# Low parts of the MLP's down weights: adding DMA and ScalarE copy in place of a VectorE subtraction

## Chip, cores and metric

The kernel runs on one core of one Trainium2 chip. The metric is device time in microseconds for one execution, taken as the median of several. The profile is of one more execution, taken by the hardware profiler.

## What is computed

A two-layer trunk over 512 tokens of width 1024, in float32. Layer 0 mixes with a gated linear recurrence, layer 1 with differential attention over a key and value projected once. Each layer ends in the squared-ReLU MLP, the part that the change touches:

```python
def squared_relu_mlp(h, w_up, w_down):
    u = jax.nn.relu(h @ w_up)
    return (u * u) @ w_down
...
ff = squared_relu_mlp(rms_norm(h, mlp_norm_pre[layer]), mlp_w_up[layer], mlp_w_down[layer])
h = h + rms_norm(ff, mlp_norm_post[layer])
```

`w_up` is 1024 x 4096 and `w_down` 4096 x 1024. The result of the MLP goes through an RMS norm with a gain before it is added to the residual stream, so turning the sign of the whole product and the sign of that gain leaves the output as it was.

## The kernel before, in words

**Split products.** TensorE multiplies in the type float32r, which keeps fewer bits than float32. Every operand is therefore held as two float32r tiles: a high part (a rounded copy) and a low part (the original less the high part). `mm3` (L192) makes each product from three matmuls: high by high, high by low, low by high. The third one, in `wmm` (L197), is the first to read the low part of the weights.

**Weights.** `load_w` (L180) brings a weight matrix in tiles of 128 x 1024 float32 (512 KB). `fetch_w` (L150) issues the load on SP's queue into the tile `raw`, of which there are four buffers for all weights. `split_w` (L161) makes the high part `whi` by a ScalarE copy (L167) and the low part `wlo` by a VectorE subtraction (L168). `whi` and `wlo` have eight buffers each. A buffer of `raw` is free again when its subtraction is done, and only then can SP issue the load that is to go into it.

**The MLP.** `block` (L377) goes through the hidden width in four quarters q of 1024 columns. For each it makes the hidden activations `u` (tiles `uhi`, `ulo`, by ScalarE's ReLU, square and copy and VectorE's subtraction) and multiplies them with that quarter of `w_down`: two halves i of 512 columns, four weight tiles each, named dn_q_i_pr.

- q = 0: the up product is plain (`up`, eight PSUM groups, each emptied by ScalarE's ReLU at L405).
- q = 1, 2, 3: four pairs p of `up_pair` (L450), a seven-product scheme. The bank `ux` takes up four products in turn and is read by ScalarE between them: L475 keeps p1 after the first and u2 after the second; L493 reads it for the last time.
- Down product, q = 0, 1, 2 (L513 to L530): half i = 0 goes through the eight row blocks kt with the four output groups n4 inside, so weight tile pr is needed from kt = 2 pr on; half i = 1 has n4 outside and needs all four tiles within its first eighth. Each n4 has a PSUM bank out of the four of the tag "mm". The fourth bank is the one that the last up group of q = 0 (L405), or the last pair's `ux` (L493), used before.
- Down product, q = 3: both halves of weights are loaded and `by_halves` (L358) goes over tokens in two halves, kt outside and eight output groups inside. Groups n = 0 to 3 use the first half's tile, n = 4 to 7 the second half's, so the fifth weight tile, dn_3_1_0, is needed with kt = 0. Groups 6 and 7 are in the bank that `ux` had.

**Order of the work.** TensorE's order is written out by a small planner. On the other engines a scheduler of the framework sets the order, by priorities and a cost model, and each engine then executes its instructions in that order: one that waits holds all behind it. GpSimd (POOL) issues the DMAs of the residual stream (L268, L337) through software-made descriptors; SP issues the weight loads.

Of the kernel before, what the change touches and what calls it, by code (L numbers as in the profile page):

```python
# [9 lines left out]
F32 = mybir.dt.float32  # L10
F32R = mybir.dt.float32r
I32 = mybir.dt.int32
U8 = mybir.dt.uint8
AF = mybir.ActivationFunctionType
# [74 lines left out]
def trunk_kernel(ctx: ExitStack, tc: tile.TileContext, x_t, w_qf, w_g, w_i, w_ao, w_k, w_q, w_v, w_bo, w_up, w_us, w_dn,  # L89
# [50 lines left out]
    ea = cp.tile([P, S], F32, name="ea")  # L140
    gnh = cp.tile([P, G_N], F32, name="gnh")
    v.tensor_scalar(gnh, gn, -0.5, None, op0=ALU.mult)
    epsc = cp.tile([P, 1], F32, name="epsc")
    v.memset(epsc, EPS)
    eps15 = cp.tile([P, 1], F32, name="eps15")
# [15 lines left out]
    def split_w(raw, gain, pr, name):  # L161

        per, ncols = raw.shape[1:]
        hi = wp.tile([P, per, ncols], F32R, tag="whi", name=f"whi_{name}_{pr}", bufs=8)
        lo = wp.tile([P, per, ncols], F32R, tag="wlo", name=f"wlo_{name}_{pr}", bufs=8)
        if gain is None:
            a.activation(hi, raw, AF.Copy)  # L167
            v.tensor_tensor(lo, raw, hi.bitcast(F32), op=ALU.subtract)  # L168
        elif gain.shape[1] == 1:
            a.activation(hi, raw, AF.Copy, scale=gain)  # L170
            v.scalar_tensor_tensor(lo, raw, gain, hi.bitcast(F32), op0=ALU.mult, op1=ALU.subtract)
        else:
            for j in range(per):
                gc = gain[:, per * pr + j:per * pr + j + 1]
                a.activation(hi[:, j, :], raw[:, j, :], AF.Copy, scale=gc)
                v.scalar_tensor_tensor(lo[:, j, :], raw[:, j, :], gc, hi[:, j, :].bitcast(F32),
                                       op0=ALU.mult, op1=ALU.subtract)
        return [(hi[:, j, :], lo[:, j, :]) for j in range(per)]

    def load_w(src, ncols, gain, name):  # L180
        out = []
        for pr in range(ncols // 128):
            out += split_w(fetch_w(src, ncols, pr, name), gain, pr, name)
        return out
# [206 lines left out]
    def block(pool, proj, gpost, name, layer, want):  # L391
# [104 lines left out]
        for q in range(4):  # L496
# [15 lines left out]
                    yield from up_pair(q, p, ts)  # L512
            if q < 3:  # L513
                for i in range(2):
                    wt = load_w(w_dn[layer, q, i], 512, None, f"dn{layer}_{q}_{i}")
                    pss = [mmt(f"dn{layer}_{q}_{i}_{n4}") for n4 in range(4)]
                    if i == 0:
                        order = [(kt, n4) for kt in range(8) for n4 in range(4)]
                    else:
                        order = [(kt, n4) for n4 in range(4) for kt in range(8)]  # L520
                    for kt, n4 in order:
                        wmm(pss[n4], wt, kt, n4 * P, uhi, ulo, 0, S, kt == 0, kt == 7)
                        if kt == 7:
                            n = 4 * i + n4
                            z = zacc[:, n, :]
                            if q == 0:
                                v.tensor_copy(z, pss[n4])
                            else:
                                v.tensor_tensor(z, pss[n4], z, op=ALU.add)  # L529
                        yield 0  # L530
            else:
                wt = [load_w(w_dn[layer, q, i], 512, None, f"dn{layer}_{q}_{i}") for i in range(2)]
                h = 0
                for r in by_halves(wt, uhi, ulo, f"dn{layer}"):
                    if isinstance(r, list):
                        spawn(bounds(pool, r, zacc, h, G_MPOST[layer], ea, want, f"m{layer}"), 0.3)
                        h += 1
                    else:
                        yield r
# [532 lines left out]
```

## Time and profile before

| what | value |
|---|---|
| median of 3 runs | 1291.78 us (1291.08 to 1293.16) |
| profiled execution | 1291.62 us |
| its span | 1289.8 us |
| mean granted TensorE clock | 0.992 |
| DMA, mean over the span | 102 GB/s, 131.01 MB |

The page gives, for each engine, its busy time and share of the span; groups of instructions by line, engine and tiles (written `out<-in`); and DMA issues with the time from issue to landing. The trace also answers with timelines (start, length, engine, line, operation, and in brackets the idle time before it and what ended it), with the chain of work that ended last, and with windows (busy time of each engine, granted clock, share and rate of the DMA engines in a stretch). The profiled execution and its span differ by 1.8 us.

### The profile page before, as it was taken

Reading aid. Unit: us, or ns where it says so; the run is one execution under the profiler, and the core shown is the slowest. Engines: PE = TensorE matmul, PEld = TensorE weight load, DVE = VectorE, ACT = ScalarE, POOL = GpSimd, SP = SyncE. Lnnn points to the kernel's source line nnn. Section 1 sums busy time; section 2 is a strip of 40 time slices with the busy share of each in tenths; the row PEclk is TensorE's granted clock in tenths of the full one; section 3 lists DMA queues with packets and bytes.
Section 4 is the critical chain, followed back from the end, with each engine's and each line's share of the span. In section 5 each row is a group of like instructions: output and inputs, shape, how many; then the busy total and the mean of one; then the engine's idle time right before and its main releaser. Section 6 shows DMA issues by size and latency. Waiting matters only on the chain.

```text
span 1289.8 us, 21392 instructions
## 1 busy us (share of the span) xinstructions
PE 1257.5 (97%) x8450; PEld 1139.5 (88%) x8450; DVE 858.2 (67%) x1791; ACT 663.9 (51%) x1333; POOL 57.4 (4%) x125
## 2 busy tenths in 40 slices
PE   9999999999999999999898999999999999999996
PEld 7989898999988989989898887889998998988995
DVE  7987777648855736647287978674875573764735
ACT  7553535247733715617265887674773370652722
POOL 0210101010000000000100000001000000000000
PEclk9999999999999999999998999999999999999998
DMA  7322222134324512513424432322433151251421
GB/s 241 112 82 66 66 66 74 59 101 152 110 99 74 180 50 66 164 33 119 176 77 155 129 100 65 99 86 78 156 107 99 33 196 33 66 164 47 138 78 66
DMA packets 40166, 131.01 MB, mean 102 GB/s; under 512 B 5089, under 2 KB 7394, under 8 KB 40066
## 3 DMA queue, kind: packets, MB, share of 16 engines
q1 hardware_dynamic: 35072, 113.52, 27.1%
q0 software_dynamic: 4752, 15.99, 4.2%
q8 instruction: 66, 1.08, 0.3%
q14 instruction: 34, 0.28, 0.1%
q10 hardware_dynamic: 242, 0.13, 0.0%
HBM read 119.93 MB, written 9.70 MB: 100 GB/s over the span
## 4 chain that ended last, share of the span: by engine, by line
PE 76%; DVE 11%; ACT 8%; DMA 2%; issue 1%; SPq 0%; DVEq 0%; ACTq 0%
PE dn L114 19%; PE up L114 7%; PE qf L114 7%; PE kq L114 6%; PE dn_h L114 5%; PE g L114 4%; PE ux L114 4%; PE v L114 3%; PE bo_h L114 3%; PE ao_h L114 3%; PE i L114 3%; PE gl L114 3%; DMA raw_dn<-in_w_dn_dram 2%; PE lg L114 2%; ACT r L409 1%
## 5 line engine op out<-in xcount | busy, mean ns | idle before, releaser
L114 PE MATMUL dn<-uhi,whi_dn 128*128 128x512 f32 x384 | 152.0, 396 | 0.0
L114 PE MATMUL dn<-ulo,whi_dn 128*128 128x512 f32 x384 | 151.9, 395 | 0.0
L114 PE MATMUL dn<-uhi,wlo_dn 128*128 128x512 f32 x384 | 151.9, 395 | 0.0
L168 DVE TENSOR_TENSOR wlo_dn<-raw_dn,whi_dn 128x1024 fp32r<-128x1024 f32 x64 | 76.7, 1220 | 18.7 <-ACT whi_dn L167 17.6
L114 PEld LDWEIGHTS dn<-uhi,wlo_dn 128*128 128x128 f32 x384 | 72.1, 188 | 17.5
L114 PEld LDWEIGHTS dn<-uhi,whi_dn 128*128 128x128 f32 x384 | 72.2, 188 | 17.5 <-issue 0.2
L114 PEld LDWEIGHTS dn<-ulo,whi_dn 128*128 128x128 f32 x384 | 72.2, 188 | 17.0
L446 ACT ACTIVATE whi_a<-raw_us 128x1024 fp32r<-128x1024 f32 x24 | 25.3, 1054 | 113.8 <-PE dn L114 113.8
L167 ACT ACTIVATE whi_dn<-raw_dn 128x1024 fp32r<-128x1024 f32 x64 | 67.0, 1054 | 16.5 <-DMA raw_dn<-in_w_dn_dram 12.9
L114 PE MATMUL dn_h<-uhi,whi_dn 128*128 128x256 f32 x240 | 68.7, 286 | 5.8 <-ACT r L493 5.8
L114 PE MATMUL up<-xhi,whi_up 128*128 128x256 f32 x256 | 72.7, 284 | 0.0
L114 PE MATMUL up<-xlo,whi_up 128*128 128x256 f32 x256 | 71.9, 281 | 0.0
L114 PE MATMUL up<-xhi,wlo_up 128*128 128x256 f32 x256 | 71.9, 281 | 0.0
L114 PE MATMUL dn_h<-ulo,whi_dn 128*128 128x256 f32 x240 | 68.1, 284 | 0.0
L114 PE MATMUL dn_h<-uhi,wlo_dn 128*128 128x256 f32 x240 | 68.0, 283 | 0.0
L529 DVE TENSOR_TENSOR zacc<-dn,zacc 128x512 f32<-128x512 f32 x32 | 22.1, 692 | 60.0 <-PE dn L114 59.9
L411 DVE TENSOR_TENSOR ulo<-r,uhi 128x1024 fp32r<-128x1024 f32 (+1 forms) x40 | 40.2, 1010 | 32.4 <-ACT uhi L410 32.4
L114 PE MATMUL ux<-xhi,whi_a 128*128 128x256 f32 x192 | 54.7, 285 | 1.8 <-DVE r L487 1.8
L114 PE MATMUL ux<-xhi,wlo_a 128*128 128x256 f32 x192 | 54.0, 281 | 0.0
L114 PE MATMUL qf<-xhi,whi_qf 128*128 128x512 f32 x128 | 53.2, 416 | 0.7 <-ACT xhi L590 0.7
L114 PE MATMUL ux<-xlo,whi_a 128*128 128x256 f32 x192 | 53.9, 281 | 0.0
L114 PE MATMUL qf<-xlo,whi_qf 128*128 128x512 f32 x128 | 50.8, 397 | 1.0 <-DVE xlo L591 1.0
(368 smaller groups left out, 4075.1 us busy)
## 6 DMA issues: line engine op xcount, KB each, us to landing
raw_dn<-in_w_dn_dram SPq DMA_DIRECT2D x64, 512.0 KB, 4.6
raw_us<-in_w_us_dram SPq DMA_DIRECT2D x48, 512.0 KB, 4.3
raw_up<-in_w_up_dram SPq DMA_DIRECT2D x16, 512.0 KB, 3.6
raw_qf<-in_w_qf_dram SPq DMA_DIRECT2D x15, 512.0 KB, 4.1
raw_wi<-in_w_i_dram SPq DMA_DIRECT2D x8, 512.0 KB, 3.9
raw_wg<-in_w_g_dram SPq DMA_DIRECT2D x8, 512.0 KB, 3.8
raw_ao<-in_w_ao_dram SPq DMA_DIRECT2D x8, 512.0 KB, 3.5
raw_wk<-in_w_k_dram SPq DMA_DIRECT2D x8, 512.0 KB, 4.6
```

The costliest lines, as they stand in the source:

```text
L114: nc.tensor.matmul(out, lhsT, rhs, **kw)
L167: a.activation(hi, raw, AF.Copy)
L168: v.tensor_tensor(lo, raw, hi.bitcast(F32), op=ALU.subtract)
L409: a.activation(r, r, AF.Square)
L411: v.tensor_tensor(ulo[pr][:, :, lo:hi], r, uhi[pr][:, :, lo:hi].bitcast(F32), op=ALU.subtract)
L446: a.activation(hi, raw, AF.Copy)
L529: v.tensor_tensor(z, pss[n4], z, op=ALU.add)
```

## The change

For the 64 tiles of the down matrix (32 in each layer) the low part is made in another way. ScalarE writes the high part with its sign turned. GpSimd issues a DMA that adds it into the raw tile within SBUF, so that `raw` becomes the original less its high part. ScalarE copies that, again with its sign turned, into `wlo`. The down products come out negative; the gain of the norm behind them, held as -0.5 times the weight in `gnh`, is made +0.5 times for its columns.

```diff
     v.tensor_scalar(gnh, gn, -0.5, None, op0=ALU.mult)
+    v.tensor_scalar(gnh[:, G_MPOST[0]:G_MPOST[1] + 8], gn[:, G_MPOST[0]:G_MPOST[1] + 8], 0.5, None, op0=ALU.mult)
...
+    def load_wn(src, ncols, name):
+        out = []
+        for pr in range(ncols // 128):
+            raw = fetch_w(src, ncols, pr, name)
+            per = raw.shape[1]
+            hi = wp.tile([P, per, ncols], F32R, tag="whi", name=f"whi_{name}_{pr}", bufs=8)
+            lo = wp.tile([P, per, ncols], F32R, tag="wlo", name=f"wlo_{name}_{pr}", bufs=8)
+            a.activation(hi, raw, AF.Copy, scale=-1.0)
+            g.dma_start(raw, hi.bitcast(F32), accum_op=ALU.add)
+            a.activation(lo, raw, AF.Copy, scale=-1.0)
+            out += [(hi[:, j, :], lo[:, j, :]) for j in range(per)]
+        return out
...
-                    wt = load_w(w_dn[layer, q, i], 512, None, f"dn{layer}_{q}_{i}")
+                    wt = load_wn(w_dn[layer, q, i], 512, f"dn{layer}_{q}_{i}")
...
-                wt = [load_w(w_dn[layer, q, i], 512, None, f"dn{layer}_{q}_{i}") for i in range(2)]
+                wt = [load_wn(w_dn[layer, q, i], 512, f"dn{layer}_{q}_{i}") for i in range(2)]
```

TensorE's and SP's instructions stand in the same order as before. VectorE loses 64 subtractions and gains one small multiplication, GpSimd's queue gains 64 DMAs, and ScalarE gains 64 copies, whose places the scheduler chose. Three places follow. In the changed kernel line numbers are 16 higher from L180 on (L405 is L421, L409 L425, L410 L426, L436 L452, L475 L491, L490 L506, L491 L507, L493 L509); L190 is its high copy, L191 the adding DMA, L192 its low copy. Tile names in these rows read whi_dn_q_i_pr and a buffer's number.

ScalarE, layer 0, at the end of the up product of q = 0, before the change; r_1_2 and r_1_3 are the ReLUs that empty the last two PSUM groups:

```order
L167 ACTIVATE whi_dn_0_0_3_3831<-raw_dn_0_0_3_3829 128x1024
L409 ACTIVATE r_1_1_3668<-r_1_1_3668 128x2x256
L410 ACTIVATE uhi_75<-r_1_1_3668 128x2x256
L405 ACTIVATE r_1_2_3722<-up_1_2_3673 128x2x256
L409 ACTIVATE r_1_2_3722<-r_1_2_3722 128x2x256
L410 ACTIVATE uhi_76<-r_1_2_3722 128x2x256
L436 ACTIVATE xhi_66<-zacc_2962 128x256
L167 ACTIVATE whi_dn_0_1_0_3941<-raw_dn_0_1_0_3939 128x1024
L436 ACTIVATE xhi_67<-zacc_2962 128x256
L436 ACTIVATE xhi_68<-zacc_2962 128x256
L167 ACTIVATE whi_dn_0_1_1_3947<-raw_dn_0_1_1_3945 128x1024
L405 ACTIVATE r_1_3_3785<-up_1_3_3727 128x2x256
```

The same place in the change, from the second low copy on (the first stands two rows ahead):

```order
L192 ACTIVATE wlo_dn_0_0_1_3822<-raw_dn_0_0_1_3819 128x1024
L192 ACTIVATE wlo_dn_0_0_2_3829<-raw_dn_0_0_2_3826 128x1024
L421 ACTIVATE r_1_2_3723<-up_1_2_3674 128x2x256
L425 ACTIVATE r_1_2_3723<-r_1_2_3723 128x2x256
L192 ACTIVATE wlo_dn_0_0_3_3836<-raw_dn_0_0_3_3833 128x1024
L426 ACTIVATE uhi_76<-r_1_2_3723 128x2x256
L452 ACTIVATE xhi_66<-zacc_2963 128x256
L190 ACTIVATE whi_dn_0_1_0_3946<-raw_dn_0_1_0_3944 128x1024
L452 ACTIVATE xhi_67<-zacc_2963 128x256
L452 ACTIVATE xhi_68<-zacc_2963 128x256
L190 ACTIVATE whi_dn_0_1_1_3953<-raw_dn_0_1_1_3951 128x1024
L421 ACTIVATE r_1_3_3786<-up_1_3_3728 128x2x256
```

All four low copies of the first half have come in ahead of the ReLU that empties the last group, three of them ahead of the ReLU before it.

ScalarE, layer 0, q = 2, the last pair of `up_pair`, before; p and u are L475's reads of ux and uz:

```order
L475 ACTIVATE p_2_3_5267<-ux_2_3_5251 128x256
L410 ACTIVATE uhi_76<-r_2_2_5127 128x1024
L475 ACTIVATE p_2_3_5281<-uz_2_3_5253 128x256
L167 ACTIVATE whi_dn_2_0_3_5374<-raw_dn_2_0_3_5372 128x1024
L475 ACTIVATE u_2_3_5295<-ux_2_3_5251 128x256
L167 ACTIVATE whi_dn_2_1_0_5484<-raw_dn_2_1_0_5482 128x1024
L167 ACTIVATE whi_dn_2_1_1_5490<-raw_dn_2_1_1_5488 128x1024
L491 ACTIVATE r_2_3_5254<-r_2_3_5254 128x256
L167 ACTIVATE whi_dn_2_1_2_5496<-raw_dn_2_1_2_5494 128x1024
L490 ACTIVATE r_2_3_5254<-r_2_3_5254 128x512
L167 ACTIVATE whi_dn_2_1_3_5502<-raw_dn_2_1_3_5500 128x1024
L493 ACTIVATE r_2_3_5254<-ux_2_3_5251 128x256
```

The same place in the change:

```order
L491 ACTIVATE p_2_3_5298<-uz_2_3_5270 128x256
L192 ACTIVATE wlo_dn_2_0_0_5374<-raw_dn_2_0_0_5371 128x1024
L491 ACTIVATE u_2_3_5312<-ux_2_3_5268 128x256
L192 ACTIVATE wlo_dn_2_0_1_5381<-raw_dn_2_0_1_5378 128x1024
L192 ACTIVATE wlo_dn_2_0_2_5388<-raw_dn_2_0_2_5385 128x1024
L190 ACTIVATE whi_dn_2_0_3_5394<-raw_dn_2_0_3_5392 128x1024
L507 ACTIVATE r_2_3_5271<-r_2_3_5271 128x256
L190 ACTIVATE whi_dn_2_1_0_5505<-raw_dn_2_1_0_5503 128x1024
L506 ACTIVATE r_2_3_5271<-r_2_3_5271 128x512
L190 ACTIVATE whi_dn_2_1_1_5512<-raw_dn_2_1_1_5510 128x1024
L509 ACTIVATE r_2_3_5271<-ux_2_3_5268 128x256
L425 ACTIVATE r_2_3_5271<-r_2_3_5271 128x1024
```

The first low copy stands ahead of the read u_2_3, and the low copies of tiles 0, 1 and 2 stand ahead of the last read of `ux` (L509, before L493). The high copies of dn_2_1_2 and dn_2_1_3, which were ahead of that read, have moved behind it. q = 1 and both quarters of layer 1 have the same sequence.

ScalarE, layer 0, q = 3, from the high copy of the fifth tile on, before:

```order
L167 ACTIVATE whi_dn_3_1_0_6144<-raw_dn_3_1_0_6142 128x1024
L167 ACTIVATE whi_dn_3_1_1_6150<-raw_dn_3_1_1_6148 128x1024
L491 ACTIVATE r_3_3_6018<-r_3_3_6018 128x256
L167 ACTIVATE whi_dn_3_1_2_6156<-raw_dn_3_1_2_6154 128x1024
L490 ACTIVATE r_3_3_6018<-r_3_3_6018 128x512
L167 ACTIVATE whi_dn_3_1_3_6162<-raw_dn_3_1_3_6160 128x1024
L493 ACTIVATE r_3_3_6018<-ux_3_3_6015 128x256
L409 ACTIVATE r_3_3_6018<-r_3_3_6018 128x1024
L410 ACTIVATE uhi_77<-r_3_3_6018 128x1024
```

and in the change:

```order
L190 ACTIVATE whi_dn_3_0_3_6166<-raw_dn_3_0_3_6164 128x1024
L507 ACTIVATE r_3_3_6043<-r_3_3_6043 128x256
L190 ACTIVATE whi_dn_3_1_0_6173<-raw_dn_3_1_0_6171 128x1024
L506 ACTIVATE r_3_3_6043<-r_3_3_6043 128x512
L190 ACTIVATE whi_dn_3_1_1_6180<-raw_dn_3_1_1_6178 128x1024
L509 ACTIVATE r_3_3_6043<-ux_3_3_6040 128x256
L425 ACTIVATE r_3_3_6043<-r_3_3_6043 128x1024
L192 ACTIVATE wlo_dn_3_0_3_6167<-raw_dn_3_0_3_6164 128x1024
L426 ACTIVATE uhi_77<-r_3_3_6043 128x1024
L192 ACTIVATE wlo_dn_3_1_0_6174<-raw_dn_3_1_0_6171 128x1024
L192 ACTIVATE wlo_dn_3_1_1_6181<-raw_dn_3_1_1_6178 128x1024
L190 ACTIVATE whi_dn_3_1_2_6187<-raw_dn_3_1_2_6185 128x1024
```

The fifth tile's low copy, wlo_dn_3_1_0, stands behind the high copy of the sixth, the last read of `ux`, a square, the fourth tile's low copy and uhi_77. On GpSimd's queue the adding DMAs of this quarter stand around four residual loads (L268, in the change L284) that come between the third and the fourth of them.

## Prediction

> **What bounds the kernel now.** I read the chain of work that ended last first, then the waits of TensorE, then timelines at the places where the change puts instructions.
>
> ```profile
> PE 76%; DVE 11%; ACT 8%; DMA 2%; issue 1%; SPq 0%; DVEq 0%; ACTq 0%
> ```
>
> ```profile
> PE dn_h L114 <- ACT r L493: 5.8, 2, 3.5
> PE v L114 <- DVE wlo_wv L176: 4.9, 2, 3.7
> PE ux L114 <- DVE r L487: 1.8, 7, 0.3
> PE ux L114 <- ACT p L475: 1.1, 1, 1.1
> ```
>
> TensorE carries the end, and it waits for little: its longest wait is for a PSUM read by ScalarE. VectorE and ScalarE matter only where TensorE waits for them. So the work that the change takes off VectorE is worth almost nothing by itself, and the question is what its replacement does to the few reads and weight tiles that TensorE needs in time.
>
> ```profile
> L168 DVE TENSOR_TENSOR wlo_dn<-raw_dn,whi_dn 128x1024 fp32r<-128x1024 f32 x64 | 76.7, 1220 | 18.7 <-ACT whi_dn L167 17.6
> ...
> L167 ACT ACTIVATE whi_dn<-raw_dn 128x1024 fp32r<-128x1024 f32 x64 | 67.0, 1054 | 16.5 <-DMA raw_dn<-in_w_dn_dram 12.9
> ```
>
> Removed: 64 subtractions of 1.22 us on VectorE. Added: 64 ScalarE copies of the form of L167, so 1.05 us each, 67 us more on ScalarE, and 64 adding DMAs of 512 KB between the two copies. On VectorE none of TensorE's waits is for `wlo_dn`; only part of the 1.8 us of L487, which stands among these subtractions, can go. I credit 1.0 us. The extra multiplication of `gnh` is a few columns at the start and costs nothing.
>
> **Price of one adding DMA.** No row shows one. The nearest:
>
> ```profile
> raw_dn<-in_w_dn_dram SPq DMA_DIRECT2D x64, 512.0 KB, 4.6
> ...
> raw_up<-in_w_up_dram SPq DMA_DIRECT2D x16, 512.0 KB, 3.6
> ...
> res_m<-rs_m POOLq DMA_DIRECT2D x8, 256.0 KB, 2.4
> ...
> bias_dr<-tb POOLq DMA_DIRECT2D x1, 1280.0 KB, 14.9
> ```
>
> ```profile
> 620.00:624.00 4.00, 0.71 (x7) 0.51 (x5) 0.10 (x1) 1.19 (x2) 0.00 (x0) 0.99 1.03 405
> 624.10:627.50 3.40, 3.31 (x16) 3.31 (x17) 2.18 (x2) 2.15 (x3) 0.00 (x0) 0.52 1.02 394
> ```
>
> The last columns are the granted clock, the DMA share and GB/s: with all engines busy the DMA moves 405 GB/s, so one pass over 512 KB takes 1.3 us. An add must read the source and the old target, two passes: 2.6 us between one add and the next when several are queued. The fixed part is 3.6 - 1.3 = 2.3 us by the quiet load, 2.4 - 0.65 = 1.75 us by the 256 KB store from GpSimd's queue, say 2.1. So an add lands **4.7 us** after the high copy, and others queue behind it at **2.6 us**. Lower bound: one pass, 1.3 us apart, landing after 3.4. Upper bound: `bias_dr`, a DMA out of SBUF from the same queue, at 14.9 / 1280 x 512 = 6.0 us for 512 KB; with it I take 7.1 us to landing and 5.0 apart. I choose the middle because tiles of 128 rows of 4 KB are like the loads, not like `bias_dr`, which reads 16 rows.
>
> The Trainium skill, "Collectives: The Full Stack", section "The bandwidth ceiling: the fold count and why AG ≠ RS ≠ AR", states that an adding DMA is slowed by its two source reads and not by the addition, from 31 to about half per engine in GB/s. With sixteen engines an estimate from that page is 2.1 us per add, and the sum below would then come to about 1308 us. No trace here shows an add, so neither this nor my value is confirmed.
>
> **Place 1: end of q = 0, both layers.**
>
> ```profile
> 344.39 2.96 ACT L167 ACTIVATE whi_dn<-raw_dn 128x1024 fp32r<-128x1024 f32 x3 [1.50 <-PE up L114]
> ...
> 358.35 0.58 ACT L405 ACTIVATE r<-up 128x512 f32<-128x512 f32 x1
> ```
>
> ```profile
> 357.96 38.50 PE dn L114 x165
> ...
> 532.73 40.37 PE dn L114 x173
> ```
>
> The high copies end at 345.4, 346.4 and 347.35, so the four adds land at 350.1, 352.7, 355.3 and 357.9; the two loads that the freed `raw` buffers let through share the engines and add up to 2.6 to the last. On ScalarE the third low copy ends at 356.4; then come a ReLU and a square (1.2), the fourth low copy (from 357.9 to 359.0, or 361.6 with the loads), uhi_76, three small `xhi` copies and two high copies (3.9 together), and the last ReLU r_1_3 (0.58), ending at 363.4 to 366.0. TensorE needs that bank for its fourth group: a down matmul takes 40.37 / 173 = 0.233 us, nine of them 2.1, so at 360.1. The wait is 3.3 to 5.9 us; I take 4.5. Before, r_1_3 ended at 358.9 and there was no wait.
>
> A long wait has a second price, the lower clock of the second window above: after the 3.48 us wait that ends at 624.19 (row below) TensorE had 0.52 of its clock for 3.4 us, which loses 3.4 x 0.48 = 1.6 us. After the wait of 2.28 us in layer 1 there was none (1.00):
>
> ```profile
> 1232.40:1235.80 3.40, 3.40 (x28) 3.40 (x29) 2.16 (x2) 2.11 (x2) 0.00 (x0) 1.00 0.00 0
> ```
>
> By these rows I charge 1.6 us to a wait of 3.5 us or more and nothing up to 2.3.
>
> The Trainium skill, "TensorE: Matmul & The Clock Gate", section "What's actually happening", puts the limit at an idle window of about 3.4 us and the low clock at one half; the trace agrees with 3.48 and 0.52.
>
> Place 1: 2 x (4.5 + 1.6) = **12.2 us**.
>
> **Place 2: last pair of q = 1 and 2, four times.**
>
> ```profile
> 519.78 1.05 ACT L167 ACTIVATE whi_dn<-raw_dn 128x1024 fp32r<-128x1024 f32 x1
> ...
> 522.60 1.06 ACT L167 ACTIVATE whi_dn<-raw_dn 128x1024 fp32r<-128x1024 f32 x1
> ...
> 527.35 0.38 ACT L475 ACTIVATE u<-ux 128x256 f32<-128x256 f32 x1
> ...
> 533.65 0.36 ACT L493 ACTIVATE r<-ux 128x256 f32<-128x256 f32 x1
> ```
>
> Count from h, the end of the first high copy (520.8); the third ends at h + 2.9. Adds land at h + 4.7, 7.3, 9.9 (to 11.5 with loads between). The first low copy goes in at h + 5.6, after p5, when its add has landed: u (L475) comes out no later than before. The third low copy ends at h + 10.9, the fourth high copy at 11.9, then a ReLU (0.4) and the high copy of tile five (1.05): 13.3. The high copy of tile six needs its load, which now waits for the second low copy (h + 8.4) and takes 4.6; with the ReLU before it (0.6) it ends at 15.0. The last read of `ux` ends at h + 15.4, or 17.0 with the loads. TensorE needs it 2.1 after the start of the down product at 532.73, h + 14.0; before it was done at 534.0, h + 13.2. Wait 1.4 to 3.0, taken as 2.2 and without the clock's price: 4 x 2.2 = **8.8 us**. Later weights have room: the down product of one half lasts over 20 us.
>
> **Place 3: q = 3, both layers.**
>
> ```profile
> 605.65 1.04 ACT L167 ACTIVATE whi_dn<-raw_dn 128x1024 fp32r<-128x1024 f32 x1
> ...
> 622.81 1.06 ACT L167 ACTIVATE whi_dn<-raw_dn 128x1024 fp32r<-128x1024 f32 x1 [3.77 <-DMA raw_dn<-in_w_dn_dram]
> 623.77 0.37 ACT L493 ACTIVATE r<-ux 128x256 f32<-128x256 f32 x1
> ```
>
> ```profile
> 624.19 0.58 PE L114 MATMUL dn_h<-uhi,whi_dn 128*128 128x256 f32 x1 [3.48 <-ACT r L493]
> ...
> 1232.40 0.38 PE L114 MATMUL dn_h<-uhi,whi_dn 128*128 128x256 f32 x1 [2.28 <-ACT r L493]
> ```
>
> TensorE waits here already: `ux`'s last read stands behind the high copy of tile eight, which waits for its load. That order is gone, and the wait with it. What is late next is the fifth tile's low copy, needed four groups into kt = 0. With h = 606.7 the chain of place 2 holds up to L509 (h + 15.4); then the square (16.5), the fourth low copy (its add lands at 11.9 + 4.7 = 16.6, up to 2.8 later for the loads, residual ones of 1 MB ahead of it on GpSimd's queue among them; ends 17.7 to 20.5), uhi_77 (21.6 at most), and the fifth low copy, ending at h + 19.9 to 23.0. TensorE went on at h + 17.5 before and has six more matmuls (0.7) to do then: +3.1 to +6.2, taken as 4.6 each. In layer 1 the old wait was 1.2 shorter and cost no clock: 1.2 + 1.6 more. Place 3: 2 x 4.6 + 2.8 = **12.0 us**. Tiles six to eight are needed 5.7 us apart and come in time.
>
> **Sum.** 12.2 + 8.8 + 12.0 - 1.0 = 32.0 us on the profiled execution's 1291.6 (median of the runs 1291.78): **1324 us**, 2.5% slower.
>
> **Rivals.**
>
> *Not slower: the adds fit into the room.* The mechanism sits in place 2 and 3: if an add lands by 3.4 us after the high copy and loads take the quiet 3.6, r_1_3 and `ux`'s read come in time, places 1 and 2 cost nothing, and the fifth low copy ends at h + 17.1. Place 3 then costs 0.3 in layer 0 and 1.5 + 1.6 in layer 1; VectorE's whole 1.8 goes, and the 1.1 of L475 may: 3.4 - 2.9, so 1292. For it: the 2.4 us stores. Against: two reads per byte. It decides from a spacing of 1.3 us down. Chance 0.12.
>
> *Much slower: adding is slow.* At 5.0 apart, 7.1 to landing, r_1_3 ends at 372.9 (wait 12.8 + 1.6, twice: 28.8), `ux`'s read at h + 22.7 (8.7 + 1.6, four times: 41), the fifth low copy at h + 32.4 (15.6 twice, + 2.8: 34): +104, 1395 us. For it: `bias_dr`'s rate. Against: the same queue's stores. Chance 0.25.
>
> *The forecast*, spacing 2.0 to 3.6: chance 0.63.
>
> **How the numbers follow.** The range leaves out the best of the first rival and the end of the second: 1300 to 1385. About 0.2% (2.6 us) is what a measurement tells from no change. The first rival's 0.12 splits around 1292 into 0.03 faster, 0.06 the same and 0.03 slower; all else is slower: 0.91.
>
> **What would show it.** Right: VectorE's busy time near 780 us and ScalarE's near 731; adds landing 4 to 6 us after issue; ScalarE waiting for them at the low copies (L192); new TensorE waits at the fourth group of dn for L421 and L509 and in dn_h for wlo_dn, with windows of half clock behind the long ones. Wrong: no TensorE wait at these reads, adds landing in under 3.4 us, or waits of over 8 us everywhere.

## The result and the profile after

The changed kernel takes **1369.7 us** (median of 3 runs, 1367.7 to 1370.9) beside 1291.78 before: ratio 1.0585, 95% interval 1.0568 to 1.0602, so 78 us or 5.9% slower where 32 us were forecast. The profiled span went from 1289.8 to 1369.1 us.

The chain of the kernel after; before, its first row began "PE 76%; DVE 11%":

```profile
PE 51%; issue 18%; DMA 11%; DVE 10%; ACT 7%; POOL 1%; SPq 0%; POOLq 0%; DVEq 0%; ACTq 0%
```

A quarter of the chain has passed from TensorE (76% to 51%) to the DMAs and the issues. The groups that the change made, on ScalarE and GpSimd, and the two DMA rows of the down weights (KB each, median us to landing):

```profile
L192 ACT ACTIVATE wlo_dn<-raw_dn 128x1024 fp32r<-128x1024 f32 x64 | 67.8, 1059 | 119.4 <-DMA raw_dn<-whi_dn 119.4
L191 POOL DMA_DIRECT2D raw_dn<-whi_dn x64 | 55.1, 866 | 577.9 <-ACT whi_dn L190 485.4
...
raw_dn<-in_w_dn_dram SPq DMA_DIRECT2D x64, 512.0 KB, 4.5
raw_dn<-whi_dn POOLq DMA_DIRECT2D x64, 512.0 KB, 7.4
```

All 64 low copies cost what was said (1.06 us), and ScalarE stood idle 119 us ahead of them. VectorE's busy time is 782.6 us (780 forecast), ScalarE's 726.4 (731). TensorE's waits in the kernel after (us in total, times, longest):

```profile
PE dn_h L114 <- ACT wlo_dn L192: 14.7, 2, 7.4
PE dn L114 <- ACT r L421: 12.4, 2, 6.4
PE dn L114 <- DVE zacc L545: 12.3, 4, 3.8
PE dn L114 <- ACT r L509: 8.7, 4, 2.4
PE ux L114 <- ACT u L491: 7.3, 5, 2.4
PE dn_h L114 <- ACT whi_dn L190: 6.9, 2, 4.0
```

Together 62.3 us; the 5.8 us of before (dn_h for L493) are gone: **+56.5 us of waits**. Behind eleven of them TensorE ran at half its clock. Some of these stretches and their sum (us, TensorE's busy time, granted clock, share of the DMA engines, GB/s):

```profile
365.78:371.40 5.62, 5.62 (x13) 0.51 1.06 189
460.10:463.50 3.40, 3.40 (x10) 0.50 1.07 202
484.73:490.80 6.07, 6.07 (x14) 0.50 0.53 173
...
1310.80:1313.30 2.50, 2.50 (x13) 0.50 0.27 105
sum 45.62, PE 45.61; mean PE 4.15
```

Length times missing clock, summed over the eleven, is 22.5 us; before had one such stretch behind the waits of the MLP, 1.6 us. So **+20.9 us of clock**, and 77.4 in all, of the 79.3 by which the span grew.

**Where the largest unforeseen wait comes from.** Layer 0, q = 1, ahead of the second half of the down product. ScalarE:

```profile
477.02 1.06 ACT L192 ACTIVATE wlo_dn<-raw_dn 128x1024 fp32r<-128x1024 f32 x1 [4.37 <-DMA raw_dn<-whi_dn]
479.48 1.06 ACT L192 ACTIVATE wlo_dn<-raw_dn 128x1024 fp32r<-128x1024 f32 x1 [1.40 <-DMA raw_dn<-whi_dn]
480.45 1.04 ACT L462 ACTIVATE whi_s<-raw_us 128x1024 fp32r<-128x1024 f32 x1
481.39 0.61 ACT L462 ACTIVATE whi_b<-raw_us 128x512 fp32r<-128x512 f32 x1
```

VectorE at the same place:

```profile
481.52 1.23 DVE L463 TENSOR_TENSOR wlo_s<-raw_us,whi_s 128x1024 fp32r<-128x1024 f32 x1 [4.72 <-ACT whi_s L462]
482.66 0.69 DVE L463 TENSOR_TENSOR wlo_b<-raw_us,whi_b 128x512 fp32r<-128x512 f32 x1
483.38 0.69 DVE L479 TENSOR_TENSOR raw_us<-raw_us,raw_us 128x512 f32<-128x512 f32 x1
483.99 2.48 DVE L545 TENSOR_TENSOR zacc<-dn,zacc 128x512 f32<-128x512 f32 x4
```

And TensorE:

```profile
484.73 0.80 PE L114 MATMUL dn<-uhi,whi_dn 128*128 128x512 f32 x1 [3.11 <-DVE zacc L545]
```

It is read backwards. TensorE wants the first half's banks for the second half; VectorE empties them at L545, but stands 4.72 us at `wlo_s`, a weight of the next quarter; its high part stands on ScalarE behind the low copies of tiles seven and eight, which wait for their adds. A wait of ScalarE has passed through VectorE to TensorE, by two queues that are each in order, though none of the data is the same. In before TensorE has no wait for zacc.

### The profile page after: what moved, and what is told of

The parts are those of the page before. It is cut to its first block, busy times and chain, and to the rows that moved or that the text cites. A ratio compares the mean times of both kernels' runs of the same rounds, so it can differ in the third digit from the quotient of the medians.

```text
span 1369.1 us, 21535 instructions
## 1 busy us (share of the span) xinstructions
PE 1281.4 (94%) x8450; PEld 1154.0 (84%) x8450; DVE 782.6 (57%) x1728; ACT 726.4 (53%) x1397; POOL 112.9 (8%) x189
## 3 DMA queue, kind: packets, MB, share of 16 engines
q1 hardware_dynamic: 35072, 113.52, 25.4%
q0 software_dynamic: 13968, 49.55, 17.2%
## 4 chain that ended last, share of the span: by engine, by line
PE 51%; issue 18%; DMA 11%; DVE 10%; ACT 7%; POOL 1%; SPq 0%; POOLq 0%; DVEq 0%; ACTq 0%
PE dn L114 15%; DMA raw_dn<-whi_dn 7%; PE kq L114 6%; PE qf L114 6%; PE dn_h L114 5%; PE g L114 4%; PE v L114 3%; DMA raw_dn<-in_w_dn_dram 3%; PE i L114 3%; PE gl L114 3%; PE lg L114 1%; ACT whi_s L462 1%; PE ao L114 1%; ACT whi_dn L190 1%; PE o L114 1%
## 5 line engine op out<-in xcount | busy, mean ns | idle before, releaser
L114 PE MATMUL dn<-uhi,whi_dn 128*128 128x512 f32 x384 | 160.8, 419 | 33.4 <-ACT r L421 12.4
L114 PE MATMUL dn<-ulo,whi_dn 128*128 128x512 f32 x384 | 158.9, 414 | 0.0
L114 PE MATMUL dn<-uhi,wlo_dn 128*128 128x512 f32 x384 | 158.6, 413 | 0.0
L192 ACT ACTIVATE wlo_dn<-raw_dn 128x1024 fp32r<-128x1024 f32 x64 | 67.8, 1059 | 119.4 <-DMA raw_dn<-whi_dn 119.4
L114 PEld LDWEIGHTS dn<-uhi,whi_dn 128*128 128x128 f32 x384 | 76.9, 200 | 56.1 <-DVE zacc L545 14.1
L191 POOL DMA_DIRECT2D raw_dn<-whi_dn x64 | 55.1, 866 | 577.9 <-ACT whi_dn L190 485.4
L114 PEld LDWEIGHTS dn<-uhi,wlo_dn 128*128 128x128 f32 x384 | 76.5, 199 | 19.0
L114 PEld LDWEIGHTS dn<-ulo,whi_dn 128*128 128x128 f32 x384 | 76.9, 200 | 18.1
L190 ACT ACTIVATE whi_dn<-raw_dn 128x1024 fp32r<-128x1024 f32 x64 | 66.0, 1046 | 9.0 <-DMA raw_dn<-in_w_dn_dram 6.0
L463 DVE TENSOR_TENSOR wlo_a<-raw_us,whi_a 128x1024 fp32r<-128x1024 f32 x24 | 29.3, 1220 | 54.7 <-ACT whi_a L462 54.7
L114 PEld LDWEIGHTS dn_h<-uhi,wlo_dn 128*128 128x128 f32 x240 | 46.6, 194 | 15.1 <-ACT wlo_dn L192 15.1
L545 DVE TENSOR_TENSOR zacc<-dn,zacc 128x512 f32<-128x512 f32 x32 | 21.0, 686 | 60.7 <-PE dn L114 60.7
```

What stands on the lines that cost most here:

```text
L114: nc.tensor.matmul(out, lhsT, rhs, **kw)
L190: a.activation(hi, raw, AF.Copy, scale=-1.0)
L191: g.dma_start(raw, hi.bitcast(F32), accum_op=ALU.add)
L192: a.activation(lo, raw, AF.Copy, scale=-1.0)
```

## The experiments

Theory 1, mine at first: the cost comes from reads and copies that stand on ScalarE behind low copies waiting for a landing. Theory 2: the adds' traffic on the DMA engines. Theory 3: the 67 us more work on ScalarE. Theory 4, beside any of these: the half clock is a cost of its own. All ratios are to before, run on the same chip.

| run | median us | ratio, 95% interval |
|---|---|---|
| after | 1369.7 | 1.0585 [1.0568, 1.0602] |
| no DMA | 1287.1 | 0.9962 [0.9949, 0.9975] |
| plain copies | 1306.7 | 1.0118 [1.0088, 1.0148] |
| adds into scratch memory | 1354.3 | 1.0483 [1.0466, 1.0500] |
| other banks | 1348.5 | 1.0443 [1.0421, 1.0464] |
| late adds, not read | 1360.6 | 1.0529 [1.0505, 1.0553] |
| reads on VectorE | 1375.3 | 1.0638 [1.0602, 1.0673] |
| filled waits | 1369.3 | 1.0596 [1.0572, 1.0621] |
| first halves only | 1329.1 | 1.0284 [1.0250, 1.0319] |
| adds of half a tile | 1327.0 | 1.0259 [1.0238, 1.0280] |
| the same, p1 on VectorE | 1313.5 | 1.0145 [1.0112, 1.0179] |
| adds of 4 KB | 1305.4 | 1.0085 [1.0052, 1.0118] |
| before, subtraction on GpSimd | 1299.7 | 1.0051 [1.0037, 1.0066] |
| before, last read on VectorE | 1286.3 | 0.9952 [0.9935, 0.9969] |
| both of these | 1289.9 | 0.9979 [0.9967, 0.9990] |

**No DMA.**

```diff
-            g.dma_start(raw, hi.bitcast(F32), accum_op=ALU.add)
```

> The kernel after without the adding DMAs: the second ScalarE copy makes each low part from the raw weights alone, so the low parts of the second matrix are left wrong; the number and shape of the matmuls and of the ScalarE copies are those of after. Theory 1 (the cost comes from reads and copies that stand on ScalarE behind low copies waiting for an add's landing): without the landing nothing is waited for there, so at most 5 us over before, 1290 to 1297 us, and 73 us or more under after. Theory 2 (the adds take bandwidth from the loads): the same time as by theory 1, since the adds are gone. Theory 3 (67 us more work on ScalarE delays the reads by itself): most of the 78 us stays, 1340 us or more.

It came out 0.4% *under* before, and under the expected 1290 to 1297 us too, with 718.7 us of work on ScalarE. Theory 3 falls: the 67 us more work delay nothing by themselves. What is left of the change gains about 5 us; TensorE's wait of 5.8 us for L493 has gone. Whether VectorE's relief does this or ScalarE's order is not shown: without the DMAs the scheduler placed the low copies otherwise than in after. Measured against this run, the adds cost not 78 but some 80 us.

**Plain copies.**

```diff
-            g.dma_start(raw, hi.bitcast(F32), accum_op=ALU.add)
+            g.dma_start(raw, hi.bitcast(F32))
```

> The kernel after with the DMA of the same shape and queue copying the negated high part over the raw tile and adding nothing; the addition is left out, so the low parts are wrong. The order of instructions is that of after. What it tells: how much of the landing time is the second read of an add. If an add costs two passes, as the prediction priced it, the copy lands 1.3 us sooner and copies queue 1.3 us apart, not 2.6: by theory 1 the waits of TensorE (62 us in after) shrink to 25 to 40 and the time is 1325 to 1345 us. If the fixed time of a DMA from GpSimd's queue is what is waited for, and not the addition, the time stays within 10 us of after. By theory 2 (bandwidth) it falls by the share of bytes that is gone, about a half of 78: 1330 us.

Same instructions in the same order on every engine, same shapes, same queue: 15 us over before instead of 76, and 18 us under the expected 1325 to 1345. TensorE's waits for the down product, 55 us in after, are 21 here; 25 to 40 of all 62 were expected. The sum of the bytes in the page is the same too (49.55 MB on GpSimd's queue), but not the time they take. While four of them are under way in after, and while they are in the run with plain copies:

```profile
346.00:356.00 10.00, 10.00 (x87) 10.00 (x86) 0.69 (x1) 5.62 (x8) 2.90 (x4) 1.00 0.97 177
```

```profile
347.00:351.00 4.00, 4.00 (x36) 4.00 (x35) 0.00 (x0) 3.99 (x6) 1.51 (x3) 1.00 0.97 375
```

The engines are as busy (0.97) and move 177 GB/s against 375: adding halves the rate. The Trainium skill, "Collectives: The Full Stack", section "The bandwidth ceiling: the fold count and why AG ≠ RS ≠ AR", has the same halving for the adding step of a ring of collectives, and this trace agrees with 177 against 375 GB/s. The step from one pass to two is worth 60 us here.

**Adds into scratch memory.**

```diff
+            scr = dr.tile([P, per, ncols], F32, tag="scr", name=f"scr_{name}_{pr}", bufs=8)
+            g.dma_start(scr, hi.bitcast(F32), accum_op=ALU.add)
...
+                v.scalar_tensor_tensor(lo, raw, -1.0, hi.bitcast(F32), op0=ALU.mult, op1=ALU.subtract)
```

> The low parts are made on VectorE again with the signs turned as in after, and the 64 adding DMAs of 512 KB from the high parts go into scratch memory outside SBUF, where nothing reads them: the same bytes on the same queue, with no reader that waits. Theory 1: near before, 1290 to 1302 us, since no copy on ScalarE waits for a landing. Theory 2 (the adds slow the loads and the GpSimd queue): most of the 78 us stays, over 1330 us.

Nobody waits for these adds, but for GpSimd once 0.3 us, and 62 us stay: over 1330 us, as theory 2 had it. An add into that memory is a dearer one (landing after 11.4 us in the median) and the weights' loads landed after 9.3 us in place of 4.6, so the run says that traffic alone can do it, but not that it does so in after. That made the next one necessary.

**Late adds, not read.**

```diff
             a.activation(hi, raw, AF.Copy, scale=-1.0)
-            g.dma_start(raw, hi.bitcast(F32), accum_op=ALU.add)
-            a.activation(lo, raw, AF.Copy, scale=-1.0)
+            v.scalar_tensor_tensor(lo, raw, -1.0, hi.bitcast(F32), op0=ALU.mult, op1=ALU.subtract)
+            g.dma_start(raw, hi.bitcast(F32), accum_op=ALU.add)
```

> The low parts are made on VectorE (signs turned as in after); behind each, the same adding DMA of 512 KB within SBUF runs from the high part into the raw tile, whose content nothing reads any more. So the adds, their bytes, their queue and the time for which a raw tile is held are those of after, and no copy waits for a landing. Theory 1 (ScalarE's reads and copies stand behind low copies that wait for a landing): the waits for L421, L509, u, zacc and the low copies go; 1290 to 1305 us. Theory 2 (the traffic of the adds slows the loads): most of the 78 us stays, over 1340 us. Between them, 1305 to 1340: the raw tiles come free later, the loads behind them start later, and the high copies on ScalarE wait for loads, as in the run with adds into scratch memory (78.7 us of such waits there, 6.0 in after); the trace would show those waits.

Theory 1 as I had it falls: no copy waits for a landing, and 68 us stay. The same place as the prediction's place 1, on ScalarE, in this run:

```profile
361.02 1.06 ACT L190 ACTIVATE whi_dn<-raw_dn 128x1024 fp32r<-128x1024 f32 x1 [5.39 <-DMA raw_dn<-in_w_dn_dram]
...
362.85 1.06 ACT L190 ACTIVATE whi_dn<-raw_dn 128x1024 fp32r<-128x1024 f32 x1 [0.16 <-DMA raw_dn<-in_w_dn_dram]
363.81 0.58 ACT L421 ACTIVATE r<-up 128x512 f32<-128x512 f32 x1
```

And in after:

```profile
350.72 1.06 ACT L192 ACTIVATE wlo_dn<-raw_dn 128x1024 fp32r<-128x1024 f32 x1 [1.74 <-DMA raw_dn<-whi_dn]
354.06 1.06 ACT L192 ACTIVATE wlo_dn<-raw_dn 128x1024 fp32r<-128x1024 f32 x1 [1.76 <-DMA raw_dn<-whi_dn]
356.54 1.06 ACT L192 ACTIVATE wlo_dn<-raw_dn 128x1024 fp32r<-128x1024 f32 x1 [1.42 <-DMA raw_dn<-whi_dn]
...
360.86 1.06 ACT L192 ACTIVATE wlo_dn<-raw_dn 128x1024 fp32r<-128x1024 f32 x1 [2.12 <-DMA raw_dn<-whi_dn]
...
365.16 0.57 ACT L421 ACTIVATE r<-up 128x512 f32<-128x512 f32 x1
```

The read that TensorE needs (L421) comes at 363.8 with nobody waiting for adds, and at 365.2 in after. What stands ahead of it is another instruction, a high copy that waits for its load, but the load waits for the same burst of DMAs: for the raw tile that the add holds, and for its share of the engines; no run tells these two apart. ScalarE's waits for these loads are 86.9 us in this run and 6.0 in after. The burst itself, four adds and three loads in after:

```profile
346.70:362.20 15.50, 8.43 (x12) 1.00 1.03 236
```

15.5 us with every DMA engine busy (share 1.03), where the prices of the prediction give 4 x 2.6 + 3 x 1.3 = 14.3. Over the whole span the two queues hold the engines 43% (25.4 and 17.2 on the page), so the mean shows nothing of it. **This is the theory that I was left with:** at a change of stage the adds and loads fill the DMA engines for 15 us and more, and everything that ScalarE has in order behind any member of that burst, add or load, comes late.

**Other banks.**

```diff
-                    pss = [mmt(f"dn{layer}_{q}_{i}_{n4}") for n4 in range(4)]
+                    pss = [(smt if i == 1 else mmt)(f"dn{layer}_{q}_{i}_{n4}") for n4 in range(4)]
```

> The kernel after, but in q = 0 to 2 the second half's four sums (i = 1) are kept in the small PSUM banks, so that its matmuls need not wait until VectorE has emptied the first half's banks. Theory 1: the four waits for zacc (12.3 us in all) go, with up to 9.6 us of half clock behind them, unless the next thing late at that place (a weight tile's low copy, or the small bank's last reader) takes their place: 15 to 22 us under after, 1348 to 1355 us. Theory 4 (the half clock costs nothing that the waits do not): 12 us under after, 1358. If what is late there is the weight tile and not the bank, no change: 1365 to 1371.

As expected: the row for `zacc` is gone from TensorE's waits and the others stand (12.6, 8.6 and 15.1 us for L421, L509 and wlo_dn). By the ratios it takes 18 us off after, by the two medians 21, where waits and clock at that place are 22.5. The largest missed term of the prediction is thereby shown to be one.

**First halves only.**

```diff
+    def load_wn(src, ncols, name, add=True):
...
+            if add:
...
+            else:
+                v.scalar_tensor_tensor(lo, raw, -1.0, hi.bitcast(F32), op0=ALU.mult, op1=ALU.subtract)
...
+                    wt = load_wn(w_dn[layer, q, i], 512, f"dn{layer}_{q}_{i}", i == 0)
```

> Only the first half's tiles (i = 0) of q = 0 to 2 are made by the adding DMA; the second half's and those of q = 3 are made on VectorE with the signs turned. Theory 1: the waits for r_1_3, the last read of ux and u stay (12.4, 8.7 and 7.3 us with some 11 us of half clock), those for zacc and in dn_h go (12.3 and 21.6 us with 13 of half clock): 35 to 40 us over before, 1327 to 1332 us. Theory 2 (bytes): 24 of 64 adds, 29 us over before, 1321 us. The waits in the trace tell more than the time: by theory 1 none for zacc and none for a low copy.

1329.1, inside the expected 1327 to 1332, and with the waits that were named: 12.6 us for the ReLU (L424 there), 9.5 for the last read of `ux`, 3.7 for u, none for zacc, none for a low copy. By number of adds (24 of 64) it would be 1321.

**Reads on VectorE.**

```diff
-            a.activation(r, ps, AF.Relu)
+            v.tensor_scalar(r, ps, 0.0, None, op0=ALU.max)
...
-            a.activation(r[:, 1, 0:256], px, AF.Relu, scale=-1.0)
+            v.tensor_scalar(r[:, 1, 0:256], px, -1.0, 0.0, op0=ALU.mult, op1=ALU.max)
```

> The kernel after with two reads of PSUM moved from ScalarE to VectorE, the ReLU r_1_3 and its like (L421) and the last read of ux (L509), so that they do not stand behind low copies. Theory 1: TensorE's waits for them (12.4 and 8.7 us) go, and the half clock behind them with them (4.3 and 6.2 us by the spacing of the matmuls): 1335 to 1350 us, if nothing else is late within 1 us of them. If the low copies or the adds hold TensorE up in another way, the waits move to another tile and the time stays over 1360.

A miss of theory 1's range by more than 25 us; the other case that was named, over 1360 with the waits at another tile, is what came. TensorE's wait for L509 did go, but the one for L421 stayed (13.3 us). VectorE in that run, at place 1:

```profile
362.56 0.69 DVE L427 TENSOR_TENSOR ulo<-r,uhi 128x512 fp32r<-128x512 f32 x1 [10.05 <-ACT uhi L426]
...
364.80 0.68 DVE L421 TENSOR_SCALAR r<-up 128x512 f32<-128x512 f32 x1
```

The read is on VectorE and as late as in after (364.80 against 365.16), for ahead of it stands `ulo`, which needs `uhi`, which stands on ScalarE behind the fourth low copy. The wait for zacc rose from 12.3 to 23.8 us. Moving one instruction off a blocked queue does not help where the other queue needs something that is still on it.

**Filled waits.**

```diff
+        def warm(n):
+            ps = smt("warm")
+            for _ in range(n):
+                nc.tensor.matmul(ps[:, 0:P], onesd, onesd, start=True, stop=True)
...
+                        if (i, kt, n4) == (0, 0, 3):
+                            warm(20 if q == 0 else 7)
+                        if (i, kt, n4) == (1, 0, 0) and q > 0:
+                            warm(10)
```

> The kernel after with small matmuls of a constant tile (128 columns, into a spare bank) put into TensorE's queue ahead of the places where it waits: 20 ahead of the fourth group of the down product at q = 0, 7 there at q = 1 and 2, and 10 ahead of the second half at q = 1 and 2. They fill the waits and compute nothing that is used. Theory 4 (the half clock behind each wait is a cost of its own, 20 us more than before): it goes at these places, and where the filling is longer than the wait it costs some tenths of a microsecond: 8 to 15 us under after, 1355 to 1362 us. If the slow matmuls behind a wait are the records' and not real, or the clock was low for another reason: 1370 us or more.

No gain by the ratio, where 8 to 15 us were expected. TensorE's waits at these places in that run (line 552 is the emptying of the banks at q = 0):

```profile
PE dn L114 <- DVE zacc L552: 9.1, 2, 5.1
...
PE dn L114 <- ACT r L509: 3.2, 4, 1.1
PE dn L114 <- ACT r L421: 2.4, 2, 1.6
```

The waits for L421 and L509 fell from 21.1 to 5.6 us, and the mean granted clock rose from 0.970 to 0.979. But a wait of 9.1 us appeared ahead of the second half at q = 0, where after has none: TensorE, quicker through the first half, only came sooner to banks that VectorE empties when the burst lets it. So the half clock is real time, but what it costs cannot be had back alone while the next thing is late as well. Theory 4 stays half open: no run here removed the low clock and nothing else.

**Adds of half a tile.**

```diff
-            g.dma_start(raw, hi.bitcast(F32), accum_op=ALU.add)
-            a.activation(lo, raw, AF.Copy, scale=-1.0)
+            g.dma_start(raw[:, 0, :], hi[:, 0, :].bitcast(F32), accum_op=ALU.add)
+            a.activation(lo[:, 0, :], raw[:, 0, :], AF.Copy, scale=-1.0)
+            v.scalar_tensor_tensor(lo[:, 1, :], raw[:, 1, :], -1.0, hi[:, 1, :].bitcast(F32), op0=ALU.mult, op1=ALU.subtract)
```

> Every tile of the second matrix still goes through the adding DMA, but only its first half (128x512, 256 KB); the low part of the other half is made on VectorE with the signs turned. ScalarE's copy of the first half waits for the landing as in after. If what the 78 us come from is the time that an add takes on the DMA engines (about 200 GB/s against about 385 for plain transfers in the windows of after and of the run with plain copies), an add of half the size is near a plain copy of the whole, which cost 15 us: 1297 to 1312 us. If it is the number of waits for a landing, or a fixed price of each, which stay 64: over 1335 us.

Between the two: 33 us over before. The down product's waits fell from 55 us to 8.2, as the bytes say, but a new one is the largest:

```profile
PE ux L114 <- ACT p L492: 22.2, 7, 4.8
```

On ScalarE, ahead of that read:

```profile
442.51 0.63 ACT L192 ACTIVATE wlo_dn<-raw_dn 128x512 fp32r<-128x512 f32 x1 [2.30 <-DMA raw_dn<-whi_dn]
443.05 1.04 ACT L426 ACTIVATE r<-r 128x1024 f32<-128x1024 f32 x1
443.99 0.36 ACT L492 ACTIVATE p<-ux 128x256 f32<-128x256 f32 x1
```

A low copy of the first tile, waiting 2.3 us for its add, has been put by the scheduler ahead of the first read of `ux` (p1), six times; in after it stands behind it. So the smaller adds lost in another place what they had saved in this one.

**The same, p1 on VectorE.**

```diff
-                a.activation(t, ps, AF.Copy)
+                (v.tensor_copy(t, ps) if name == "p1" else a.activation(t, ps, AF.Copy))
```

> The run with adds of half a tile, with one more edit: the first read of ux in each pair (p1) is made on VectorE, so that it does not stand on ScalarE behind the first low copy. The adds, their bytes and their number stay. If the place in ScalarE's queue is what costs there (that run's TensorE waited 22.2 us for this read, with 11.4 us of half clock behind it at six places, and lost 33 us to before), the time falls by 25 to 33 us: 1294 to 1302 us. If the adds hold the kernel up in whatever order, the wait moves to the next read (u or the last read of ux) and the time stays over 1315.

Half a hit: 15 us of the expected 25 to 33, and 1313.5 lies just under the bound of the other theory. The wait for p1 is gone; u, the next read behind the same low copy, takes its place with 9.8 us, and the weights of q = 3 are late by 8.9. The place in the queue costs, but moving one read of a row of reads moves the wait to the next one.

**Adds of 4 KB.**

```diff
-            g.dma_start(raw, hi.bitcast(F32), accum_op=ALU.add)
+            g.dma_start(raw[:, 0, 0:8], hi[:, 0, 0:8].bitcast(F32), accum_op=ALU.add)
```

> The kernel after with the adding DMA cut to the first 8 elements of each row (4 KB in all instead of 512 KB), so that the low parts are left wrong but for these. The order, the 64 issues on GpSimd and the 64 waits of ScalarE for a landing stay; the time on the DMA engines goes. If the bytes make the cost, 1286 to 1296 us, like the run without any DMA (1287). If the fixed time of an issue and a landing makes most of it, over 1310 us, no less than the run with plain copies of 512 KB (1307).

1305: above the expected 1296 for "only bytes", under the 1310 for "only the fixed time". From issue to landing, of all DMAs at the raw tiles, loads among them, it took

```profile
DMA to landing us min/median/max: 2.0/3.4/6.1
```

and the one wait left in the down weights' neighbourhood over 5 us is again p1's, behind a low copy that comes ahead of it:

```profile
PE ux L114 <- ACT p L491: 12.8, 7, 2.3
```

In after that copy stands behind p1: against the expectation, ScalarE's order did not stay that of after. With next to no bytes the kernel takes 11 us over before and 16 over no DMA at all (0.9962 to 1.0085), but these 16 cannot be put down to the 64 waits for a landing: most of TensorE's waiting here is for p1, and comes by the new order. Full plain copies, in the order of after, cost 15 over before, adds 76. So of the 80 us between the run without DMAs and after, 60 are shown to come with the addition's second pass; how the other 20 divide between landing, bytes and order stays open.

**Two versions of before.** The subtractions of `w_dn` on GpSimd (one edit at L168, for these tiles), and the last read of `ux` on VectorE:

```diff
-            v.tensor_tensor(lo, raw, hi.bitcast(F32), op=ALU.subtract)
+            (g if pool else v).tensor_tensor(lo, raw, hi.bitcast(F32), op=ALU.subtract)
```

```diff
-            a.activation(r[:, 1, 0:256], px, AF.Relu, scale=-1.0)
+            v.tensor_scalar(r[:, 1, 0:256], px, -1.0, 0.0, op0=ALU.mult, op1=ALU.max)
```

> The kernel before with the 64 subtractions of the second matrix's low parts on GpSimd, no DMA and no turned signs. GpSimd's products of 128x256 take 0.73 us in before, so a subtraction of 128x1024 some 2.9 us: VectorE is relieved as in after and nothing on ScalarE waits for a low part. Theory 1 and the run without adds (1287 us): 1285 to 1292. A raw tile is held 1.7 us longer than by VectorE; if that alone makes the loads and the high copies late, as where the adds hold the raw tiles: 1300 us or more.

> The kernel before with one read moved: the last read of ux (L493) is made on VectorE, so that it does not stand behind a high copy on ScalarE that waits for its load. TensorE's longest wait of before (5.8 us, two times, with 1.2 us of half clock) should shrink to under 2: 1286 to 1289 us. If VectorE reaches the read no sooner, because it stands behind low parts or squares that need ScalarE: 1291 to 1293.

> The two kernels above in one: the subtractions on GpSimd and the last read of ux on VectorE, which then has room. If both gain by themselves, 1282 to 1287 us; if the subtractions on GpSimd already take the wait for the read away, the same as with them alone; if GpSimd's subtractions hold the raw tiles too long, 1300 us or more.

GpSimd takes 2.52 us for one subtraction, holds the raw tile longer, and ScalarE's high copies wait 27.7 us for loads (12.9 in before): 0.5% slower, at 1299.7 us just under the 1300 named for the slow case and over the 1285 to 1292 of the other. TensorE waits 7.5 us for the last read of `ux` at four places where it has no wait in before: it looks like a milder form of the same chain. With the read moved too it is 0.2% under before, between the cases that were named. The read alone is the best of all and inside its forecast: **1286.3 us, 0.5% under before** and 6% under after, with TensorE's 5.8 us of wait at that place down to 2.5 (under 2 was expected). Nothing in these runs suggests a use for the adding DMA: without any price for the low parts (the run without DMAs) the kernel is no faster than with this one read moved.

## Why the prediction was wrong in its size

The direction, the waits named at the three places and the two passes of an add were right; the sum had 32 us where the trace has 77. The measured 1369.7 us lies inside the stated 1300 to 1385, but that is luck: the upper end was drawn for the slow adds of the second rival (1395), which did not come, and what filled the gap stood in neither account.

**Price of an add: two passes, as forecast, but too low among other transfers.** Forecast 4.7 us from the high copy to landing and 2.6 apart; at the 177 GB/s of the window above, 512 KB take 2.96 us. In the first burst the low copies start 5.6 us after the first high copy (which ends at 345.1), then 3.3, 2.5 and 4.3 apart (rows of the late-adds section), the last with loads between. At places 2 and 3, where loads run beside the adds, the first of them lands 7.2 to 8.6 us after its high copy. The sign named for being right, landing 4 to 6 us after issue, was not met: the median is 7.4. Neither of the other prices was the case. With one pass, which is what a plain copy takes, the kernel still needs 1307 us, 15 more than the first rival's 1292; and the slow price of the second rival would have had r_1_3 end at 372.9, where it ended at 365.7, near the upper end of the forecast 363.4 to 366.0.

**Place 1: 12.2 forecast, 17.0 measured.** Waits of 12.4 us in two, not 9; the clock behind them took 4.6, not 3.2, for the low clock lasted 5.6 and 3.6 us, not 3.4 each time.

**Place 2, the last read of `ux`: 8.8 forecast, 13.8 measured.** The four waits are 8.7, as worked out, but by two errors that cancel: at q = 2 (h = 539.4) the read ended at h + 17.2, over the bounds of 15.4 to 17.0, and TensorE came to its place at h + 15.2, not 14.0, held up by u. "Nothing up to 2.3" for the clock was wrong: three of the four were followed by half clock. Two of them, one quarter of the hidden width apart, on TensorE's timeline:

```profile
459.51 0.50 PE L114 MATMUL dn<-uhi,whi_dn 128*128 128x512 f32 x1 [1.98 <-ACT r L509]
...
556.61 0.50 PE L114 MATMUL dn<-uhi,whi_dn 128*128 128x512 f32 x1 [2.00 <-ACT r L509]
```

The first is followed by half clock (460.10 above), the second by none. What differs is where they fall. In this trace the granted clock is halved for 3.41, 6.83 or 10.24 us at a time, and its changes all lie on one grid of 3.41 us. TensorE in stretches of that grid, around the first wait and around the second:

```profile
456.67:460.08 3.41, 1.43 (x7) 1.00 0.93 232
460.08:463.50 3.42, 3.42 (x10) 0.50 1.09 205
...
552.24:555.65 3.41, 2.37 (x12) 1.00 0.90 290
555.65:559.07 3.42, 2.46 (x11) 1.00 1.04 195
559.07:562.48 3.41, 3.41 (x16) 1.00 1.09 207
```

The first wait lies within one stretch and leaves 1.43 of its 3.41 us busy: the next stretch has half the clock. The second is split over two, which keep 2.37 and 2.46 us busy, and the clock stays. In all of after, a stretch at full clock with up to 0.42 of its time busy was followed by half clock, and none with 0.51 or more was. Before's 2.28 us without a price, on which the rule stood, was split in the same way (2.03 and 2.52 us busy in the stretches from 1228.10 on). So the place of a wait on the grid decides, not its length alone, and for waits of about 2 us that is chance.

The Trainium skill, "TensorE: Matmul & The Clock Gate", section "What's actually happening", gives an idle window of about 3.4 us as the condition, and says that the window runs free of the kernel's start; this trace agrees with the length of the window and that it runs free, but a window with 1.43 us busy was enough, so by measurement the condition is not a wait of 3.4 us.

**The failed step, place 2: "Later weights have room: the down product of one half lasts over 20 us."** I had looked only for the weights of the down product itself. What was late after these 20 us was not one of them but the emptying of the banks (L545) behind `wlo_s`, behind `whi_s`, behind the low copies of tiles seven and eight: 12.3 us of waits and 10.2 of half clock, 22.5 of the 45 missing. The run with other banks took it away and gained 18 to 21. With it goes **"u (L475) comes out no later than before"**, 7.3 us. The first low copy stands ahead of u, as read, but its add landed at h + 7.2 where 4.7 was forecast, so that the copy could not go in at h + 5.6. In after, ScalarE at q = 2:

```profile
546.59 1.06 ACT L192 ACTIVATE wlo_dn<-raw_dn 128x1024 fp32r<-128x1024 f32 x1 [1.56 <-DMA raw_dn<-whi_dn]
547.55 0.37 ACT L491 ACTIVATE u<-ux 128x256 f32<-128x256 f32 x1
```

**Place 3: 12.0 forecast, 16.8 measured.** "That order is gone, and the wait with it" was wrong as well: after q = 3 begins, a high copy waits for its load as before, and the fifth low copy follows later than the bounds. In after, ScalarE:

```profile
642.54 1.06 ACT L192 ACTIVATE wlo_dn<-raw_dn 128x1024 fp32r<-128x1024 f32 x1 [1.57 <-DMA raw_dn<-whi_dn]
...
652.73 1.06 ACT L190 ACTIVATE whi_dn<-raw_dn 128x1024 fp32r<-128x1024 f32 x1 [2.85 <-DMA raw_dn<-in_w_dn_dram]
...
660.60 1.06 ACT L192 ACTIVATE wlo_dn<-raw_dn 128x1024 fp32r<-128x1024 f32 x1 [0.30 <-DMA raw_dn<-whi_dn]
```

The first high copy of this stage ended at 635.3 (h). The first low copy ends at 643.6 and sets a raw tile free; the load of tile five lands in it 9.1 us later, in the midst of adds, the residual loads and other weight loads, where the prediction had no wait of a high copy for it. That copy ends at h + 18.5, not 13.3, and the fifth low copy at h + 26.4, not 19.9 to 23.0.

**The credit: 1.0 forecast, 0.3 measured** where it was looked for. The run without DMAs shows 5 us, by the wait for L493, which the prediction had counted as gone for another reason.

Together 17.0 + 13.8 + 22.5 + 7.3 + 16.8 - 0.3 = 77.1. Of the 45 missing, 22.5 and 7.3 are steps that failed, 5 the clock rule, 9.6 terms that were mis-sized by the burst of loads and adds (4.8 at place 1, 4.8 at place 3), and 0.7 the credit.

## What to carry to other kernels

Price a transfer by the burst it falls into, not by its mean share: here 43% of the DMA engines over the span was 100% for 15 us at the first change of stage, and 97% for the 34 us from 540.00 on at a later one. Then follow each engine's queue past the instruction that waits, and past the engine: list everything that stands in order behind it up to the end of the burst, whatever data it uses, and ask of each who needs it; the largest cost here was two queues away from the add. Where such a wait is to be taken away, moving the one read that is seen late only pays if nothing ahead of it in its new queue hangs on the old one.

## What the hardware showed that was not expected

- An adding DMA within SBUF moves 177 GB/s where a plain one moves 375, with the engines equally busy. GpSimd takes 0.87 us to issue it and 0.53 for a plain one of the same shape.
- Half clock on TensorE came behind waits of 1.98, 2.19 and 2.30 us, and did not come behind others of 2.00 and 2.28: the former lay so that they left 0.42 or less of one stretch of a fixed grid of 3.41 us busy, the latter were split over two stretches with 0.59 or more each. It was granted for 3.41, 6.83 or 10.24 us, part of which could lie within the wait.
- An adding DMA of 512 KB from SBUF into scratch memory took 11.4 us in the median, against 7.4 within SBUF.
